# A hybrid decoder step on one core: the mixer's blocks in pairs, its small TensorE runs joined, the skip term on ScalarE

## The chip, the cores and the metric

One Trainium2 chip, one of its cores. The metric is device time in microseconds of one execution of the whole program, median over runs. TensorE multiplies matrices into PSUM, VectorE and ScalarE work on tiles in SBUF and PSUM, GpSimd (POOL) does small work and issues some DMAs, SyncE (SP) issues the rest.

## The reference

One layer of a decoder is applied to 256 prompt tokens and to 8 sample tokens (one new token each, with caches), with the same weights, all float32:

```
proj = rms_norm(x) @ w_in                  # q | k | v | z | x,B,C | dt, 6688 columns
attn = windowed GQA over 16 heads of 64, with q/k norm and per-head sinks
xbc  = silu(causal_dwconv(xbc, width 4))
y    = ssd_scan(xs, dt, a, B, C)           # two chunks of 128 tokens, 32 heads, state 128
y    = y + xs * d_skip                     # the skip term
y    = rms_norm(y * silu(z))
x    = x + concat(attn, y) @ w_out
x    = x + cross attention into 256 memory tokens
x    = x + conv FFN                        # 2048 -> 2 x 5632 -> 2048
```

Beside the two activations, the caches and states after the step are returned. For the sample tokens the scan is one step: y = C . (old state * decay) + ..., so each sample's old state (32 heads x 64 x 128) is multiplied by C and summed.

## The kernel before

Activations are kept transposed: 128 features on the partitions, 264 tokens (256 prompt, 8 sample) along the columns. Each large product is computed as three TensorE products of a high and a low part in the type fp32r (`mm3`, lines 104 to 106). Weights come in parts of 128 x 1024 on SP's queue; ScalarE writes the high part (line 89), VectorE the low part (line 90), four buffers each. `proj` accumulates two blocks of 128 output features at a time in two PSUM banks, both over the whole of a weight part before the next part, and then has each bank evacuated at high priority. There are three banks under the tag "mm", two under "t", one each under "s", "x" and "y".

The mixer is the stretch from the first input projection to the output projection. `in_pair` is called once per pair of 128-column blocks of w_in, 96 matmuls each, in the order k, v, q, B, C, x, z. Around these matmuls, the small work is issued:

- Scan decays (lines 477 to 506): cumulated log decays `la` come from a product with a triangle of ones, [128 tokens, 64]; a second pair of products, lines 481 and 482, computes the same transposed, 32 partitions wide, for a copy to DRAM (`dram_la`) that the scan later reads back broadcast.
- The sums of squares of q (lines 617 to 620): eight products, 32 outputs wide, go to four column groups of TensorE (`pq[32 * j:...]`).
- Attention of the first 128 queries (`attn_first`, four calls of two blocks each) and of the second 128 (`attn_prompt`, eight calls): logits, a softmax on VectorE and ScalarE, transposes, copy into `pt`, then value matmuls with 64 outputs (lines 602 and 564), copied to `attn`. Small fp32 products run as two passes each, so a call of four value matmuls shows 8 instructions.
- Sample attention (`attn_sample`): its small tiles `es_e` and `dgs` share the three buffers "h0" with the attention's probabilities and with the old states of `ssd_sample`.
- `conv_pair`: each evicted block goes into one of four single tiles `u` of a ring (`next_u`); the last 11 columns are copied to `cnew`, four taps are accumulated (line 748 on ScalarE, 750 on VectorE), then tanh.
- `ssd_prompt(g)`: for a group of 8 heads and each chunk: decays on ScalarE (814, 815), transposes of xs, value-like products (830, 64 outputs, 16 passes), the skip term and the sum on VectorE in four instructions (833), carry terms (838, 846).
- `ssd_sample(g)`: 8 loads of old states and 2 broadcasts on GpSimd's queue, 8 products (874) and 8 sums (875) on VectorE.
- `z_pair`: the gate, per block of 256 columns: tanh on ScalarE (905), two instructions on VectorE (906, 907), sum of squares, split into high and low part.

The order of work on every engine is made by a planner that simulates the engines and takes what is ready by priority, earlier in the program first. `issue_after(x)` holds the instructions of its block behind x on their engine. The engines then run their queues in order.

Of the kernel before, what the change touches and what calls it, by code (L numbers as in the profile page):

```python
# [7 lines left out]
F32 = mybir.dt.float32  # L8
F32R = mybir.dt.float32r
AF = mybir.ActivationFunctionType  # L10
ALU = mybir.AluOpType
# [5 lines left out]
TP, TS = 256, 8  # L17
T = TP + TS
# [30 lines left out]
def hybrid_decoder_step_kernel(ctx: ExitStack, tc: tile.TileContext, I, O):  # L49
    nc = tc.nc  # L50
# [10 lines left out]
    def psum(tag):  # L61
        return ps.tile([128, 512], F32, tag=tag, name=tag, bufs=banks[tag])
# [38 lines left out]
    marks = {}  # L101
# [166 lines left out]
    def pc(name, i=0, n=1):  # L268
        o = _PC[name][0]
        return par[:, o + i:o + i + n]  # L270
# [159 lines left out]
    p = psum("y")  # L430
# [49 lines left out]
    PE.matmul(p[:, 64:128], ones, dtan2, start=True, stop=True)  # L480
    for c in range(2):
        PE.matmul(p[0:32, 128 + c * 128:256 + c * 128], dtan[:, c, :], tri, start=True, stop=True)
    la = mp.tile([128, 64], F32, name="la")
# [9 lines left out]
    ring = []  # L493
    for i in range(4):
        u = mp.tile([128, 3 + T], F32, name=f"u{i}")
        P.memset(u[:, 0:3], 0.0)
        ring.append(u)
    ringn = [0]

    def next_u():  # L500
        ringn[0] += 1
        return ring[ringn[0] % 4]

    laT = next_u()[0:32, 3:259]
    V.tensor_copy(out=laT, in_=p[0:32, 128:384])
    nc.sync.dma_start(out=dram_la.rearrange("c h l -> h c l"), in_=laT.rearrange("p (c l) -> p c l", c=2))
    dsm = mp.tile([32, 2, 8], F32, name="dsm")
# [16 lines left out]

    def attn_prompt(j, rq, nrq, c):

# [29 lines left out]
        for h in range(2):  # L556
            for kb in range(nb):
                tr(p[:, (h * nb + kb) * 128:(h * nb + kb) * 128 + 128], e[:, h, kb * 128:kb * 128 + 128])
        pt = mp.tile([128, 4, 128], F32, tag="bc", name="pt", bufs=2)
        S.copy(out=pt[:, 0:2 * nb, :], in_=p[:, 0:2 * nk].rearrange("p (a q) -> p a q", q=128))  # L560
        o = psum("t")
        for h in range(2):
            for kb in range(nb):
                PE.matmul(o[64 * h:64 * h + 64, 0:128], vn[:, kb, pp, 64 * h:64 * h + 64], pt[:, h * nb + kb, :],
                          start=kb == 0, stop=kb == nb - 1)
        marks["attn"] = S.copy(out=attn[:, j, c * 128:c * 128 + 128], in_=o[:, 0:128])

    def attn_first(j):
# [28 lines left out]
        pt = mp.tile([128, 4, 128], F32, tag="bc", name="pt", bufs=2)  # L597
        S.copy(out=pt, in_=p.rearrange("p (a q) -> p a q", q=128))
        o = psum("t")
        for i in range(4):  # L600
            h = i % 2
            PE.matmul(o[64 * h:64 * h + 64, 128 * (i // 2):128 * (i // 2) + 128], vn[:, 0, pp, 64 * h:64 * h + 64], pt[:, i, :], start=True, stop=True)
        S.copy(out=attn[:, j:j + 2, 0:128], in_=o[:, 0:256].rearrange("p (i q) -> p i q", i=2))

# [12 lines left out]
    pq = psum("s")  # L617
    for d in range(2):
        for j in range(4):
            PE.matmul(pq[32 * j:32 * j + 32, 0:TP], nw[:, d, :], qsq[d][:, j, :TP], start=d == 0, stop=d == 1)  # L620
    cpc = mp.tile([128, 24, 8], F32, name="cpc")
# [28 lines left out]
    def second_chunk(pp):  # L650
# [6 lines left out]
        for h, (hs, ho) in enumerate(halves):  # L657
# [3 lines left out]
            V.tensor_tensor(out=qs[pp][ho, :, h, :], in0=x, in1=hi.bitcast(F32), op=ALU.subtract)  # L661

    for j in range(0, 8, 2):
        attn_first(j)
    for j in range(8):
        if j % 4 == 0:
            second_chunk(j // 4)
        d = 2 * (j // 4)
        attn_prompt(j, rqs[:, :, j % 4, d:d + 2], nrqs[:, :, j % 4, d:d + 2], 1)

    def attn_sample():
# [26 lines left out]
        S.activation(out=es, in_=sk, func=AF.Exp, bias=mx)  # L698
        e = mp.tile([128, 129], F32, tag="h0", name="es_e", bufs=3)
        S.activation(out=e, in_=p[:, 0:129], func=AF.Exp, bias=mx, accum_out=den)  # L700
# [5 lines left out]
        V.tensor_copy(out=zdiag(1)[:, :, :, 0:8], in_=p[:, 0:128].rearrange("p (j t c) -> p t j c", j=4, c=8))  # L706
        dg = mp.tile([128, 128], F32, tag="h0", name="dgs", bufs=3)
        V.tensor_scalar(out=dg, in0=ident, scalar1=e[:, 128:129], scalar2=None, op0=ALU.mult)
# [27 lines left out]

    def conv_blk(bi, pm):
        u = next_u()
        V.tensor_tensor(out=u[:, 3:], in0=pm, in1=r0, op=ALU.mult)
        return u  # L740

    def conv_side(b0, us, dst):
        c = mp.tile([128, 2, TP], F32, tag="c", name="c", bufs=2)
        for m, u in enumerate(us):
            bi = b0 + m
            V.tensor_copy(out=cnew[:, bi, :], in_=u[:, TP:])
# [18 lines left out]
    def conv_pair(b0, dst):  # L765
        us = []
        in_pair(lambda m, pm: us.append(conv_blk(b0 + m, pm)))
        conv_side(b0, us, dst)
# [28 lines left out]
    def ssd_prompt(g):  # L797
        hs = slice(8 * g, 8 * g + 8)
        hp = mp.tile([128, 512], F32, tag="hp", name="hp", bufs=1)
        for c in range(2):  # L800
# [31 lines left out]
            for i in range(4):  # L832
                V.scalar_tensor_tensor(out=x[:, i, :], in0=x[:, i, :], scalar=pc("d_skip", 4 * g + i), in1=y[:, i * 128:i * 128 + 128],
                                       op0=ALU.mult, op1=ALU.add)
            if c == 1:
# [54 lines left out]
    def z_pair(i):  # L890
        zs = []

        def ev(m, pm):
            z = next_u()[:, 3:]
            V.tensor_tensor(out=z, in0=pm, in1=r0, op=ALU.mult)
            V.tensor_copy(out=zsam[:, 2 * i + m, :], in_=z[:, TP:])
            zs.append(z[:, :TP])

        in_pair(ev)
        for m in range(2):  # L900
            k = 2 * i + m
            z = zs[m]
            y = xs[k // 4][:, k % 4, :TP]
            th = small.tile([128, T], F32, tag="raw", name="th")[:, :TP]
            S.activation(out=th, in_=z, func=AF.Tanh, scale=0.5)
            V.tensor_tensor(out=y, in0=z, in1=y, op=ALU.mult)
            V.scalar_tensor_tensor(out=y, in0=th, scalar=1.0, in1=y, op0=ALU.add, op1=ALU.mult)
            sumsq(accy[:, :TP], y, k == 0, TP, V)
            split(Y[k // 8][0][:, k % 8, :TP], Y[k // 8][1][:, k % 8, :TP], y, gssd[:, k:k + 1])
# [24 lines left out]

    conv_group(0)
    conv_group(1)
    ssd_prompt(0)
    conv_group(2)
    ssd_sample(0)
    ssd_prompt(1)  # L940
# [648 lines left out]
```

## Time and profile before

| | |
|---|---|
| median of 3 runs | 1386.8 us (1386.02 to 1387.09) |
| profiled execution | 1386.54 us, span 1384.3 us |
| TensorE busy | 1376.5 us, 99% of the span, 11415 matmuls |
| weight loads busy | 1348.3 us, 97% |
| VectorE busy | 1048.7 us, 76% |
| ScalarE busy | 766.1 us, 55% |
| GpSimd busy | 94.8 us, 7% |
| granted TensorE clock | full in all 40 slices |
| DMA | 298.31 MB, 215 GB/s in the mean |

Share is of the span. A fp32 product appears as two instructions per matmul; matmuls are pipelined, so an instruction's listed duration (some 0.28 us) is longer than the distance between two starts.

### The profile page before, as it was taken

To read this page: it belongs to the slowest core of one execution; us is meant where nothing else is said; L and a number is where in the kernel's file an instruction comes from. 1 tells how busy PE (TensorE), PEld (TensorE's weight loads), DVE (VectorE), ACT (ScalarE), POOL (GpSimd) and SP (SyncE) were. 2 spreads that over 40 slices of the span, in tenths; PEclk is the share of its full clock that TensorE was granted. 3 is DMA by queue.
4 is the path that set the end of the run, shared out by engine and by line. 5 is a ranking of instruction groups with operands and counts; after the bars stand their busy time and mean duration, and the time that the engine had idled before them with its cause. 6 is when DMAs were issued, how large, how long until landed. Compare 5 with 4: busy or idle time off the path is not lost.

```text
span 1384.3 us, 28768 instructions
## 1 busy us (share of the span) xinstructions
PE 1376.5 (99%) x11415; PEld 1348.3 (97%) x11415; DVE 1048.7 (76%) x1865; ACT 766.1 (55%) x1261; POOL 94.8 (7%) x286
## 2 busy tenths in 40 slices
PE   9999999999999999999999999999999999999999
PEld 8999999999999999889999999999999999999998
DVE  7979799999987774478777775777577757765655
ACT  7667755556545555476565544554455445543532
POOL 0000011111000000002010000000000000000000
PEclk9999999999999999999999999999999999999999
DMA  7954467777677566766576765676667656655664
GB/s 296 331 163 135 145 209 254 232 245 259 234 220 239 182 240 211 308 219 193 187 256 216 259 210 188 214 255 214 186 214 244 196 185 198 198 183 185 192 188 139
DMA packets 89477, 298.31 MB, mean 215 GB/s; under 512 B 12032, under 2 KB 17152, under 8 KB 88832
## 3 DMA queue, kind: packets, MB, share of 16 engines
q1 hardware_dynamic: 83840, 277.61, 60.6%
q0 software_dynamic: 5504, 18.88, 4.2%
q8 instruction: 89, 1.46, 0.4%
q14 instruction: 44, 0.36, 0.1%
HBM read 280.77 MB, written 16.23 MB: 215 GB/s over the span
## 4 chain that ended last, share of the span: by engine, by line
PE 97%; DMA 1%; DVE 1%; ACT 0%; issue 0%; SPq 0%; ACTq 0%
PE mm L105 21%; PE mm L104 20%; PE mm L106 20%; PE t L105 10%; PE t L106 9%; PE t L104 9%; PE t L245 1%; PE t L283 1%; PE y L830 1%; DMA wraw<-in_w_co_dram 1%; PE y L846 0%; DMA open<-in_open_dram 0%; PE x L283 0%; DVE wlo L90 0%; PE s L245 0%; PE mm L245 0%
## 5 line engine op out<-in xcount | busy, mean ns | idle before, releaser
L89 ACT CAST whi<-wraw 128x1024 fp32r<-128x1024 f32 x440 | 459.5, 1047 | 518.2 <-PE mm L105 278.3
L90 DVE TENSOR_TENSOR wlo<-wraw,whi 128x1024 fp32r<-128x1024 f32 x440 | 540.7, 1231 | 220.8 <-ACT whi L89 214.9
L105 PE MATMUL t<-x2l,whi 128*128 128x264 f32 x704 | 200.6, 285 | 0.0
L105 PE MATMUL mm<-x2l,whi 128*128 128x264 f32 x704 | 200.5, 285 | 0.0
L105 PE MATMUL mm<-hl,whi 128*128 128x264 f32 x704 | 199.6, 285 | 0.0
L106 PE MATMUL t<-x2h,wlo 128*128 128x264 f32 x704 | 199.1, 283 | 0.0
L106 PE MATMUL mm<-x2h,wlo 128*128 128x264 f32 x704 | 198.7, 283 | 0.0
L106 PE MATMUL mm<-hh,wlo 128*128 128x264 f32 x704 | 197.6, 282 | 0.0
L104 PE MATMUL mm<-x2h,whi 128*128 128x264 f32 x704 | 196.5, 279 | 0.4 <-DVE res L1285 0.4
L104 PE MATMUL t<-x2h,whi 128*128 128x264 f32 x704 | 196.4, 279 | 0.0
L104 PE MATMUL mm<-hh,whi 128*128 128x264 f32 x704 | 194.1, 280 | 0.0
L104 PE MATMUL mm<-xh,whi 128*128 128x264 f32 x576 | 163.8, 286 | 0.0
L105 PE MATMUL mm<-xl,whi 128*128 128x264 f32 x576 | 163.5, 285 | 0.0
L106 PE MATMUL mm<-xh,wlo 128*128 128x264 f32 x576 | 162.1, 286 | 0.0
L104 PEld LDWEIGHTS mm<-x2h,whi 128*128 128x128 f32 x704 | 132.3, 188 | 0.6 <-ACT whi L89 0.6
L104 PEld LDWEIGHTS t<-x2h,whi 128*128 128x128 f32 x704 | 132.3, 188 | 0.0
L106 PEld LDWEIGHTS t<-x2h,wlo 128*128 128x128 f32 x704 | 132.1, 188 | 0.0
L106 PEld LDWEIGHTS mm<-x2h,wlo 128*128 128x128 f32 x704 | 132.1, 188 | 0.0
L106 PEld LDWEIGHTS mm<-hh,wlo 128*128 128x128 f32 x704 | 131.9, 188 | 0.0
L105 PEld LDWEIGHTS mm<-hl,whi 128*128 128x128 f32 x704 | 131.7, 187 | 0.0
L105 PEld LDWEIGHTS mm<-x2l,whi 128*128 128x128 f32 x704 | 131.7, 187 | 0.0
L105 PEld LDWEIGHTS t<-x2l,whi 128*128 128x128 f32 x704 | 131.7, 187 | 0.0
(497 smaller groups left out, 2893.8 us busy)
## 6 DMA issues: line engine op xcount, KB each, us to landing
wraw<-in_w_up_dram SPq DMA_DIRECT2D x176, 512.0 KB, 4.4
wraw<-in_w_in_dram SPq DMA_DIRECT2D x96, 512.0 KB, 4.7
wraw<-in_w_dn_dram SPq DMA_DIRECT2D x88, 512.0 KB, 4.4
wraw<-in_w_out_dram SPq DMA_DIRECT2D x48, 512.0 KB, 4.3
h<-in_h_dram POOLq DMA_DIRECT2D x32, 256.0 KB, 4.6
hn<-in_h_dram SPq DMA_DIRECT2D x16, 512.0 KB, 4.8
out_state_s_dram<-hn POOLq DMA_DIRECT2D x16, 512.0 KB, 3.6
e<-dram_la SPq DMA_DIRECT2D x16, 256.0 KB, 4.8
```

Source lines behind the costliest of these rows:

```text
L89: S.copy(out=hi, in_=x)
L90: V.tensor_tensor(out=lo, in0=x, in1=hi.bitcast(F32), op=ALU.subtract)
L104: PE.matmul(out, wh, xh, start=start, stop=False)
L105: PE.matmul(out, wh, xl, start=False, stop=False)
L106: return PE.matmul(out, wl, xh, start=False, stop=stop)
L245: PE.matmul(first[c][:, :T], pre[k // 2][i][:, k % 2, c * 128:(c + 1) * 128], A[k // 8][x][:, k % 8, :], start=k + i + x == 0, stop=k == K ...
L283: return PE.transpose(out, in_, cst[0:k, C_ID:C_ID + k])
L830: PE.matmul(y[o:o + 64, (h // 2) * 128:(h // 2) * 128 + 128], xdt[:, h, :], es[h // 4][:, h % 4, :], start=True, stop=True)
```

## The change

- The two 32-wide products of line 482 go; `la` is transposed by TensorE instead ([128, 64] to [64, 128]) and that is copied to DRAM.
- The ring has two tiles of two blocks instead of four of one; evictions of a pair go into one tile. Copies to `cnew` and `zsam`, and the gate's tanh and VectorE instructions, handle both blocks at once. The gate's tanh tile has the tag "c" instead of "raw".
- The sums of squares of q are issued with the product that needs the last square first, the seven others behind it.
- `attn_first` and `attn_prompt` return `pt`; value matmuls of two calls are issued together, the one that needs the later `pt` first, the rest behind it, with one copy to `attn`. The `pt` of blocks 2, 3, 6 and 7 in the second half take the buffers "hp" and "cb" instead of "bc".
- The skip term: ScalarE scales xs by d_skip in place (four instructions), VectorE adds the PSUM bank in one.
- `es_e` and `dgs` become slices of a tile in the buffer "hp" instead of "h0".
- `ssd_sample(0)` comes right behind `conv_group(0)`, ahead of `conv_group(1)`; it stood behind `conv_group(2)`.

```diff
-    for c in range(2):
-        PE.matmul(p[0:32, 128 + c * 128:256 + c * 128], dtan[:, c, :], tri, start=True, stop=True)
...
-    for i in range(4):
-        u = mp.tile([128, 3 + T], F32, name=f"u{i}")
-        P.memset(u[:, 0:3], 0.0)
+    for i in range(2):
+        u = mp.tile([128, 2, 3 + T], F32, name=f"u{i}")
+        P.memset(u[:, :, 0:3], 0.0)
         ring.append(u)
...
-    laT = next_u()[0:32, 3:259]
-    V.tensor_copy(out=laT, in_=p[0:32, 128:384])
-    nc.sync.dma_start(out=dram_la.rearrange("c h l -> h c l"), in_=laT.rearrange("p (c l) -> p c l", c=2))
+    laT = next_u()[0:64, 0, 3:131]
+    p = psum("x")
+    tr(p[0:64, 0:128], la)
+    V.tensor_copy(out=laT, in_=p[0:64, 0:128])
+    nc.sync.dma_start(out=dram_la.rearrange("c h l -> (c h) l"), in_=laT)
...
+    def second_values(j, pts):
+        pp = j // 4
         o = psum("t")
...
+        def value(a, h, kb):
+            return PE.matmul(o[64 * h:64 * h + 64, 128 * a:128 * a + 128], vn[:, kb, pp, 64 * h:64 * h + 64], pts[a][:, 2 * h + kb, :],
+                             start=kb == 0, stop=kb == 1)
+
+        with tc.issue_after(value(1, 0, 0).ins):
+            for x in [(a, h, kb) for a in (1, 0) for h in range(2) for kb in range(2)][1:]:
+                value(*x)
+        marks["attn"] = S.copy(out=attn[:, j:j + 2, 128:TP], in_=o[:, 0:256].rearrange("p (i q) -> p i q", i=2))
...
+    def first_values(pp, pts):
...
+        with tc.issue_after(value(1, 0).ins):
+            for a, i in [(a, i) for a in (1, 0) for i in range(4)][1:]:
+                value(a, i)
+        S.copy(out=attn[:, 4 * pp:4 * pp + 4, 0:128], in_=o.rearrange("p (i q) -> p i q", i=4))
...
-    for d in range(2):
-        for j in range(4):
-            PE.matmul(pq[32 * j:32 * j + 32, 0:TP], nw[:, d, :], qsq[d][:, j, :TP], start=d == 0, stop=d == 1)
+
+    def q_sums(d, j):
+        return PE.matmul(pq[32 * j:32 * j + 32, 0:TP], nw[:, d, :], qsq[d][:, j, :TP], start=d == 1, stop=d == 0)
+
+    with tc.issue_after(q_sums(1, 3).ins):
+        for d in (1, 0):
+            for j in range(4):
+                if (d, j) != (1, 3):
+                    q_sums(d, j)
...
+    for pp in range(2):
+        first_values(pp, [attn_first(4 * pp + 2 * a) for a in range(2)])
     for j in range(0, 8, 2):
-        attn_first(j)
-    for j in range(8):
         if j % 4 == 0:
             second_chunk(j // 4)
         d = 2 * (j // 4)
-        attn_prompt(j, rqs[:, :, j % 4, d:d + 2], nrqs[:, :, j % 4, d:d + 2], 1)
+        second_values(j, [attn_prompt(x, rqs[:, :, x % 4, d:d + 2], nrqs[:, :, x % 4, d:d + 2], 1, tag)
+                          for x, tag in zip((j, j + 1), ("bc", "bc") if j % 4 == 0 else ("hp", "cb"))])
...
-                V.scalar_tensor_tensor(out=x[:, i, :], in0=x[:, i, :], scalar=pc("d_skip", 4 * g + i), in1=y[:, i * 128:i * 128 + 128],
-                                       op0=ALU.mult, op1=ALU.add)
+                S.activation(out=x[:, i, :], in_=x[:, i, :], func=AF.Copy, scale=pc("d_skip", 4 * g + i))
+            V.tensor_tensor(out=x, in0=x, in1=y.rearrange("p (i l) -> p i l", i=4), op=ALU.add)
...
+        zs = next_u()
+        in_pair(lambda m, pm: V.tensor_tensor(out=zs[:, m, 3:], in0=pm, in1=r0, op=ALU.mult))
+        V.tensor_copy(out=zsam[:, 2 * i:2 * i + 2, :], in_=zs[:, :, 3 + TP:])
+        z = zs[:, :, 3:3 + TP]
+        y2 = xs[i // 2][:, 2 * (i % 2):2 * (i % 2) + 2, :TP]
+        th = mp.tile([128, 2, TP], F32, tag="c", name="th", bufs=2)
+        S.activation(out=th, in_=z, func=AF.Tanh, scale=0.5)
+        V.tensor_tensor(out=y2, in0=z, in1=y2, op=ALU.mult)
+        V.scalar_tensor_tensor(out=y2, in0=th, scalar=1.0, in1=y2, op0=ALU.add, op1=ALU.mult)
...
     conv_group(0)
+    ssd_sample(0)
     conv_group(1)
     ssd_prompt(0)
     conv_group(2)
-    ssd_sample(0)
     ssd_prompt(1)
```

## Rows read from the trace of the kernel before

**Rows 1.** Stretches: us, then busy us (instructions) of PE, PEld, DVE, ACT, POOL; clock, DMA.

```profile
160.00:200.00 40.00, 40.00 (x383) 38.73 (x382) 31.46 (x76) 26.20 (x46) 4.47 (x8) 1.00 0.59 185
...
280.00:320.00 40.00, 40.00 (x337) 39.21 (x337) 40.00 (x85) 25.41 (x51) 6.86 (x7) 1.00 0.75 235
...
560.00:700.00 140.00, 137.10 (x1144) 130.91 (x1133) 102.82 (x177) 82.26 (x133) 12.92 (x33) 1.00 0.64 223
```

**Rows 2.** TensorE's waits: waited for, us in total, times, longest us; first of six.

```profile
PE x L206 <- DVE eps L279: 1.2, 1, 1.2
```

**Rows 3.** TensorE in order of time, a value run: start us, duration us, instruction, count.

```profile
107.49 0.28 PE L106 MATMUL mm<-xh,wlo 128*128 128x264 f32 x1
107.70 0.66 PE L602 MATMUL t<-pt,vn 128*64 128x128 f32 x8
...
108.52 0.28 PE L105 MATMUL mm<-xl,whi 128*128 128x264 f32 x1
```

**Rows 4.** TensorE in order of time, a run of 16 passes in the scan.

```profile
259.88 0.28 PE L105 MATMUL mm<-xl,whi 128*128 128x264 f32 x1
260.09 1.09 PE L830 MATMUL y<-e,xdt 128*64 128x128 f32 x16
...
261.34 0.28 PE L104 MATMUL mm<-xh,whi 128*128 128x264 f32 x1
```

**Rows 5.** TensorE in order of time, the sums of squares of q.

```profile
81.22 0.28 PE L106 MATMUL mm<-xh,wlo 128*128 128x264 f32 x1
81.43 1.06 PE L620 MATMUL s<-qsq,zz 128*32 128x256 f32 x12
...
82.64 0.29 PE L105 MATMUL mm<-xl,whi 128*128 128x264 f32 x1
...
83.37 0.28 PE L105 MATMUL mm<-xl,whi 128*128 128x264 f32 x1
...
84.35 0.29 PE L104 MATMUL mm<-xh,whi 128*128 128x264 f32 x1
```

**Rows 6.** TensorE in order of time, the log decays.

```profile
79.46 0.28 PE L104 MATMUL mm<-xh,whi 128*128 128x264 f32 x1
...
80.07 0.62 PE L482 MATMUL x<-cst,dtan 128*32 128x128 f32 x4
...
80.85 0.29 PE L106 MATMUL mm<-xh,wlo 128*128 128x264 f32 x1
```

**Rows 7.** TensorE in order of time, the transpose of a narrow tile.

```profile
155.09 0.28 PE L105 MATMUL mm<-xl,whi 128*128 128x264 f32 x1
155.21 0.27 PE L283 MATMUL x<-cst,bcs 128*32 128x128 f32 x1
...
155.44 0.28 PE L104 MATMUL mm<-xh,whi 128*128 128x264 f32 x1
```

**Rows 8.** VectorE from 70 to 420 us by line: busy us, mean ns, idle before.

```profile
L833 DVE SCALAR_TENSOR_TENSOR xs<-xs,par,y 128x128 f32<-128x128 f32 x32 | 9.1, 337 | 0.0
...
L907 DVE SCALAR_TENSOR_TENSOR xs<-th,xs 128x256 f32<-128x256 f32 x16 | 6.4, 410 | 0.0
...
L746 DVE COPY cnew<-u 128x11 f32<-128x11 f32 x24 | 3.9, 163 | 0.0
...
L843 DVE TENSOR_TENSOR ti<-y,ti 128x512 f32<-128x512 f32 x4 | 2.7, 677 | 0.0
```

**Rows 9.** ScalarE from 70 to 420 us by line, the scan's decays.

```profile
L814 ACT ACTIVATE e<-e,la 128x128 f32<-128x128 f32 x64 | 20.2, 391 | 17.0 <-DMA e<-dram_la 12.7 <-DVE xs L833 4.3
```

**Rows 10.** Old states of the samples, 160 to 260 us: waits ended by loads, landing times.

```profile
  DMA h<-in_h_dram: 0.9, 1
...
DMA to landing us min/median/max: 3.6/4.3/6.8
```

**Rows 11.** VectorE in order of time, the last gated sample rows.

```profile
412.61 0.35 DVE L97 TENSOR_TENSOR yl<-ysam,yh 128x64 fp32r<-128x64 f32 x2
```

**Rows 12.** TensorE in order of time, the second half of the output projection begins.

```profile
413.44 0.48 PE L104 MATMUL mm<-yh,whi 128*128 128x264 f32 x1
```

More of the change, by code (lines that the diff above doesn't have):

```diff
@@ L501, in next_u @@
         ringn[0] += 1
-        return ring[ringn[0] % 4]
-    laT = next_u()[0:32, 3:259]
-    V.tensor_copy(out=laT, in_=p[0:32, 128:384])
-    nc.sync.dma_start(out=dram_la.rearrange("c h l -> h c l"), in_=laT.rearrange("p (c l) -> p c l", c=2))
+        return ring[ringn[0] % 2]
+    laT = next_u()[0:64, 0, 3:131]
[3 more added lines that the diff above has]
+    nc.sync.dma_start(out=dram_la.rearrange("c h l -> (c h) l"), in_=laT)
     dsm = mp.tile([32, 2, 8], F32, name="dsm")
@@ L523, in hybrid_decoder_step_kernel, with attn_prompt @@
     V.tensor_scalar(out=nsink, in0=pc("sink_p", 0, 16), scalar1=-1.0, scalar2=None, op0=ALU.mult)
-    def attn_prompt(j, rq, nrq, c):
+    def attn_prompt(j, rq, nrq, c, tag):
         pp = j // 4
@@ L558, in attn_prompt @@
                 tr(p[:, (h * nb + kb) * 128:(h * nb + kb) * 128 + 128], e[:, h, kb * 128:kb * 128 + 128])
-        pt = mp.tile([128, 4, 128], F32, tag="bc", name="pt", bufs=2)
+        pt = mp.tile([128, 4, 128], F32, tag=tag, name="pt", bufs=2 if tag == "bc" else 1)
         S.copy(out=pt[:, 0:2 * nb, :], in_=p[:, 0:2 * nk].rearrange("p (a q) -> p a q", q=128))
+        return pt
+    def second_values(j, pts):
+        pp = j // 4
         o = psum("t")
[L562 to L566, printed above, removed]
+        def value(a, h, kb):
[5 more added lines that the diff above has]
+        marks["attn"] = S.copy(out=attn[:, j:j + 2, 128:TP], in_=o[:, 0:256].rearrange("p (i q) -> p i q", i=2))
     def attn_first(j):
@@ L598, in attn_first, with value @@
         S.copy(out=pt, in_=p.rearrange("p (a q) -> p a q", q=128))
+        return pt
+    def first_values(pp, pts):
         o = psum("t")
-        for i in range(4):
+        def value(a, i):
             h = i % 2
-            PE.matmul(o[64 * h:64 * h + 64, 128 * (i // 2):128 * (i // 2) + 128], vn[:, 0, pp, 64 * h:64 * h + 64], pt[:, i, :], start=True, stop=True)
-        S.copy(out=attn[:, j:j + 2, 0:128], in_=o[:, 0:256].rearrange("p (i q) -> p i q", i=2))
+            c = 256 * a + 128 * (i // 2)
+            return PE.matmul(o[64 * h:64 * h + 64, c:c + 128], vn[:, 0, pp, 64 * h:64 * h + 64], pts[a][:, i, :], start=True, stop=True)
+        with tc.issue_after(value(1, 0).ins):
+            for a, i in [(a, i) for a in (1, 0) for i in range(4)][1:]:
+                value(a, i)
+        S.copy(out=attn[:, 4 * pp:4 * pp + 4, 0:128], in_=o.rearrange("p (i q) -> p i q", i=4))
     qsq = [T3(apool, 4, tag="R", name=f"qsq{i}", bufs=4) for i in range(2)]
@@ L698, in attn_sample @@
         S.activation(out=es, in_=sk, func=AF.Exp, bias=mx)
-        e = mp.tile([128, 129], F32, tag="h0", name="es_e", bufs=3)
+        own = mp.tile([128, 512], F32, tag="hp", name="own", bufs=1)
+        e = own[:, 0:129]
         S.activation(out=e, in_=p[:, 0:129], func=AF.Exp, bias=mx, accum_out=den)
@@ L706, in attn_sample @@
         V.tensor_copy(out=zdiag(1)[:, :, :, 0:8], in_=p[:, 0:128].rearrange("p (j t c) -> p t j c", j=4, c=8))
-        dg = mp.tile([128, 128], F32, tag="h0", name="dgs", bufs=3)
+        dg = own[:, 256:384]
         V.tensor_scalar(out=dg, in0=ident, scalar1=e[:, 128:129], scalar2=None, op0=ALU.mult)
@@ L735, in hybrid_decoder_step_kernel @@
     cnew = mp.tile([128, 24, 11], F32, name="cnew")
[L737 to L740, printed above, removed]
     def conv_side(b0, us, dst):
         c = mp.tile([128, 2, TP], F32, tag="c", name="c", bufs=2)
-        for m, u in enumerate(us):
+        V.tensor_copy(out=cnew[:, b0:b0 + 2, :], in_=us[:, :, TP:])
+        for m in range(2):
+            u = us[:, m, :]
             bi = b0 + m
-            V.tensor_copy(out=cnew[:, bi, :], in_=u[:, TP:])
             w = [cwh[:, i * 24 + bi:i * 24 + bi + 1] for i in range(4)]
@@ L765, in conv_pair @@
     def conv_pair(b0, dst):
-        us = []
-        in_pair(lambda m, pm: us.append(conv_blk(b0 + m, pm)))
+        us = next_u()
+        in_pair(lambda m, pm: V.tensor_tensor(out=us[:, m, 3:], in0=pm, in1=r0, op=ALU.mult))
         conv_side(b0, us, dst)
@@ L890, in z_pair @@
     def z_pair(i):
[L891 to L899, printed above, removed]
+        zs = next_u()
[7 more added lines that the diff above has]
+        V.scalar_tensor_tensor(out=y2, in0=th, scalar=1.0, in1=y2, op0=ALU.add, op1=ALU.mult)
         for m in range(2):
             k = 2 * i + m
[L902 to L907, printed above, removed]
+            y = y2[:, m, :]
             sumsq(accy[:, :TP], y, k == 0, TP, V)
```

## The prediction

> **What bounds the kernel now.** I read the stretches first, then TensorE's waits, then the order of time around the places that the diff touches. In the stretches TensorE is busy for the whole 40.00 us of each of the 13 stretches from 40 to 560 us, of which two stand in [rows 1]; the mixer, which is all that the diff edits, lies inside. Busy alone proves little, since ends of matmuls are modelled. So I looked at the waits: the longest single wait of TensorE anywhere is 1.2 us, and none of its waits lies between 40 and 560 us [rows 2]. Then at starts in order of time: projection matmuls start 0.12 us apart there, and wherever the distance is larger, another TensorE instruction stands between. The mixer's length is therefore the sum of what TensorE issues. VectorE is second: 31.46 us busy of 40 in 160 to 200, but 40.00 in 280 to 320 [rows 1]. It is full there without delaying TensorE.
>
> What does cost TensorE something beside its columns is a change of shape. A run of value matmuls (output 64 partitions wide, 8 passes) begins 0.21 us after the last projection matmul instead of 0.12 [rows 3], and the first projection matmul behind it is stretched as well. So I price a run from the start of the last projection matmul ahead to the start of the second one behind, minus two steps of 0.12.
>
> **The change, part by part.**
>
> *Value runs.* One run of 8 passes: 108.52 - 107.49 - 0.24 = 0.79 us [rows 3]. A run of 16 passes of the same shape stands in the scan: 261.34 - 259.88 - 0.24 = 1.22 us [rows 4]. Two runs joined into one save 2 x 0.79 - 1.22 = 0.36. The first half of the queries has 4 runs and gets 2: 2 x 0.36 = 0.72 us. The second half has 8 and gets 4; nearly all of these 8 touch a run of transposes and share an end with it, which I put at 0.04 a run (no row prices it alone), so 4 x (2 x 0.75 - 1.22) = 1.1 us if the new ones stand alone and 4 x 0.36 = 1.4 if all do; I take 1.2. The run is ordered so that its first matmul needs the later of the two probability tiles; the rest is queued behind that one and cannot be split off.
>
> *Query sums.* Today these are three runs. The first (12 passes): 82.64 - 81.22 - 0.24 = 1.18. The second (2 passes): 84.35 - 83.37 - 0.24 = 0.74, and the third is its like at 85.9 us [rows 5]. Together 2.66. Eight products of 32 outputs go to four column groups, which work beside each other: the 12 passes are four rounds, the last two half full, and 16 passes fill the same four rounds. So I take 1.20 for the single run. Gain 1.46 us. The run now waits for the last square; what follows it (the norms of q) already waited for that.
>
> *Log-decay transposed.* The run at 79.46 us costs 80.85 - 79.46 - 0.24 = 1.15 us, of which the two 32-wide products hold everything from 80.07 on [rows 6]. Less the 0.09 that their own entry takes (0.21 - 0.12, as above), a projection matmul could start at 79.98 in their place and the next at 80.10: 80.10 - 79.46 - 0.24 = 0.40 us for what stays. The new transpose of `la` has its nearest row in that of `bcs`, 32 columns wide: 155.44 - 155.09 - 0.24 = 0.11 us, entered after 0.12 us like a projection matmul [rows 7]. I take that: gain 1.15 - 0.40 - 0.11 = 0.64. From the other side, if it changed shape as the value runs do, it costs 0.1 more on each side, gain 0.44. The Trainium skill says of this ("TensorEngine Tiling (Array Packing)", Key Properties) that changing the tiling mode drains the engine, which for an output of 64 partitions would be that 0.2; by it the sum below would be 3.8 instead of 4.0. The row disagrees for a transpose, the value runs agree. The transpose waits for VectorE's copy of `la` and takes its PSUM bank only when the three readers of the former tile are done; behind it waits only the DMA of `la` to DRAM, which is read for the decays of the scan, after attention.
>
> *Skip term, pairs, small copies: no TensorE time, priced as cover.* VectorE loses 32 instructions with 9.1 us and gets 8 additions of 512 columns at 0.68 (as the product from PSUM at line 843): -3.7 us. Copies into `cnew`: 24 become 12, -1.9; those into `zsam` 16 become 8 at the same rate, -1.1; the two gate instructions 16 become 8 each, 6.4 to about 5.4 for the second and a little less for the first, -1.6 [rows 8]. In all some 8 us less on VectorE. ScalarE gets 32 scalings of 128 columns; the decay rows are of that shape, 0.39 us each and 20.2 / 64 = 0.32 where they follow each other [rows 9], so 10 to 12.5 us. What hides this is the room on ScalarE, 25.41 us busy of 40 where VectorE is full [rows 1]. If the cover is gone, the price is a wait of the following VectorE addition behind ScalarE's queue; see the rivals.
>
> *Old states of group 0 ahead of the second convolution.* Same instructions, earlier: 8 products and 8 sums of about 0.68 us, 8 loads and 2 broadcasts on GpSimd's queue. The loads shared their buffers with the small tiles of the sample rows, and that wait goes. What is late next is the broadcast of C, whose one buffer now holds the probabilities of the seventh and eighth block. The earlier work falls into 160 to 200 us, where VectorE has 8.5 us free [rows 1]. Behind it in VectorE's order stand evictions and weight splits; behind it on GpSimd's queue, the first group's carry product and addition, needed only at the gate.
>
> *The ring of two double tiles* holds what four single ones held; the first half of a pair now also waits for readers of the other half, two pairs (2 x 96 x 0.12 = 23 us) earlier. Taken as nothing; bound: one eviction late by a VectorE instruction, 0.7 us, once.
>
> **Sum.** 0.72 + 1.2 + 1.46 + 0.64 = 4.0 us, against the profiled execution's own 1386.54 us (span 1384.3): 1382.5. The median of the runs is 0.26 above that execution, so 1382.8. The bounds above give 3.6 to 4.3. One split of the scan's 16-pass runs more or fewer (the last block has two runs of 8) moves it by 0.36 either way, and the 2.9 us that TensorE is idle in 560 to 700 us can move if the order on the engines comes out differently. The likeliest case's own range is thus 1381.0 to 1384.0.
>
> **Rivals.**
>
> *A: the gain comes back at the end of the mixer.* The second half of the output projection begins at 413.44 us [rows 12], and VectorE begins to deliver the last gated sample rows at 412.61 [rows 11]. If VectorE sets that moment, a TensorE that arrives 4.0 us sooner waits 4.0 - 0.8 = 3.2 us there, and the time is 1386.0. For: VectorE is full in 200 to 400. Against: its load falls by 8 us in that same stretch, and the runs that shrink lie before 170 us, where it has room.
>
> *B (slower): VectorE blocked on early states.* An in-order VectorE that waits for a state load holds up an eviction; two output banks follow each other, so an eviction may be 24 matmuls, 24 x 0.12 = 2.9 us, late before TensorE stops. The loads landed in 3.6 us at the least, 4.3 in the middle and 6.8 at worst [rows 10]. If all 8 moved products waited out the difference to the median, 8 x 2.5 = 20 us, less the 8.5 free, 11.5 us fall on TensorE; less 4.0: 1394.3. It decides from the point where a wait exceeds 2.9 us. Against: only one wait of 0.9 us for such a load stands in the stretch [rows 10]. The Trainium skill states a mechanism for late loads ("SBUF — State Buffer", the box on the "DVE blocks DMA" trap): descriptors of a DMA issued on GpSimd's queue are written by GpSimd, which is locked out while certain VectorE instructions run. The 6.8 in a stretch with VectorE full is in its favour, the median of 4.3 is not.
>
> *C (slower): VectorE's skip addition behind ScalarE.* ScalarE's queue holds weight conversions that wait for buffers. Were each of the 8 additions late enough to cost TensorE 1 us beyond those 2.9, the time is 1386.8 - 4.0 + 8 = 1390.8.
>
> *D: the edit does less than it says,* other TensorE work being set between the passes of a joined run, so that only sums and transpose gain: 2.1 us, 1384.7.
>
> **How the numbers follow.** Within 0.2% (2.8 us) nothing can be told from no change, so faster means below 1384.0, slower above 1389.6. Forecast 0.65; A 0.12 and D 0.09 fall inside 0.2%; B 0.06 and C 0.05 above; 0.03 for an order on the engines that changes stages the diff does not touch, either way. Faster 0.67, same 0.22, slower 0.11. The range reaches from 1380.8 over A and D to 1387.0 and leaves out B and C and the tails.
>
> **What would show it.** Right: value runs of 16 passes, 2 and 4 of them; one run of 16 for the query sums, near 1.2 us; no 32-wide product near 80 us; the first matmul of the up-projection and every later stage 4 us earlier, by the end of attention already; VectorE below 39 us in the 40 us stretches that were full. Wrong: a wait of TensorE between 40 and 560 us, above all on an eviction or on the last gated rows, or joined runs with projection matmuls between their passes.

## The result and the profile after

After: 1389.38 us median (12 runs, 1385.76 to 1392.04), before 1386.59 (12 runs, 1385.65 to 1387.12): ratio 1.0022, interval 1.0013 to 1.0030. The change made the kernel slower by 2.8 us where 4.0 less were forecast. The profiled execution of after, which the rows below describe, is the slowest of its runs: 1392.04 us, span 1389.8. The runs of after lie 6.3 us apart and those of before 1.5, so the waits below are those of one execution, 2.7 us above the median.

TensorE after, in order of time (start us, duration us, instruction, count): query sums with the transpose of `la`, then a joined value run, against [rows 3, 5 to 7].

```profile
83.78 0.28 PE L104 MATMUL mm<-xh,whi 128*128 128x264 f32 x1
83.91 0.27 PE L283 MATMUL x<-cst,la 128*64 128x128 f32 x1
83.93 0.37 PE L105 MATMUL mm<-xl,whi 128*128 128x264 f32 x1
84.23 1.07 PE L637 MATMUL s<-qsq,zz 128*32 128x256 f32 x16
85.23 0.39 PE L106 MATMUL mm<-xh,wlo 128*128 128x264 f32 x1
85.46 0.28 PE L104 MATMUL mm<-xh,whi 128*128 128x264 f32 x1
...
109.97 0.28 PE L104 MATMUL mm<-xh,whi 128*128 128x264 f32 x1
110.18 1.09 PE L615 MATMUL t<-pt,vn 128*64 128x128 f32 x16
...
111.43 0.28 PE L106 MATMUL mm<-xh,wlo 128*128 128x264 f32 x1
```

The first six rows hold three steps of 0.12 us: 85.46 - 83.78 - 0.36 = 1.32 us for the transpose and the sums (1.31 forecast). The value run costs 111.43 - 109.97 - 0.24 = 1.22, as forecast. At the last projection matmul ahead of the sample attention, TensorE is 4.76 us ahead of before (168.02 against 172.78; 0.44 of it from an earlier start). Compared at the same projection matmul, those that before issues at 170 to 175 us, after is 4.40 us ahead, 3.95 without its earlier start: the whole forecast gain. It is lost in the mixer. The stretches of after, columns as in [rows 1]:

```profile
160.00:200.00 40.00, 38.64 (x367) 37.02 (x366) 33.73 (x71) 25.63 (x45) 5.90 (x11) 1.00 0.63 209
200.00:240.00 40.00, 39.05 (x327) 37.12 (x327) 39.41 (x77) 21.99 (x43) 4.83 (x9) 1.00 0.72 242
240.00:280.00 40.00, 36.82 (x304) 35.34 (x302) 37.24 (x65) 23.30 (x44) 6.56 (x8) 0.98 0.72 221
280.00:320.00 40.00, 40.00 (x318) 38.33 (x319) 36.28 (x64) 24.40 (x46) 7.80 (x9) 0.93 0.62 202
```

TensorE is idle in three of them, and in 280 to 320 us it is busy with 318 matmuls instead of the 337 of [rows 1], at a granted clock of 0.93. Its waits between 150 and 420 us, where before has none [rows 2]:

```profile
PE mm L104 <- ACT whi L89: 3.2, 1, 3.2
PE mm L106 <- DVE wlo L90: 2.3, 3, 1.0
```

The three waits on the low part of a weight, at 185, 190 and 204 us, follow VectorE standing at the early state products. VectorE's stops of 160 to 260 us by what ended them, then VectorE in order of time:

```profile
DVE h L895 <- DMA cb<-dram_bc: 4.1, 2, 2.2
```

```profile
181.02 1.30 DVE L895 TENSOR_TENSOR h<-h,cb 128x512 f32<-128x512 f32 x2 [2.17 <-DMA cb<-dram_bc]
182.23 0.88 DVE L771 SCALAR_TENSOR_TENSOR c<-u,par,c 128x256 f32<-128x256 f32 x2
...
185.37 1.22 DVE L90 TENSOR_TENSOR wlo<-wraw,whi 128x1024 fp32r<-128x1024 f32 x1
...
197.51 1.29 DVE L895 TENSOR_TENSOR h<-h,cb 128x512 f32<-128x512 f32 x2 [1.88 <-DMA cb<-dram_bc]
```

TensorE meets that split (start us, duration us, instruction, and in brackets the idle time before it):

```profile
185.42 0.28 PE L105 MATMUL mm<-xl,whi 128*128 128x264 f32 x1
186.64 0.39 PE L106 MATMUL mm<-xh,wlo 128*128 128x264 f32 x1 [0.94 <-DVE wlo L90]
```

VectorE stands 2.17 us for the broadcast of C and then works off what is queued. The split begins at 185.37 and ends at 186.59, when TensorE has already stood for it 0.94 us. The longest wait comes through ScalarE, at the decays of the scan. ScalarE, then TensorE:

```profile
266.63 1.06 ACT L89 CAST whi<-wraw 128x1024 fp32r<-128x1024 f32 x1 [0.86 <-DMA wraw<-in_w_in_dram]
274.42 2.45 ACT L835 ACTIVATE e<-e,la 128x128 f32<-128x128 f32 x8 [6.73 <-DMA e<-dram_la]
276.77 1.03 ACT L89 CAST whi<-wraw 128x1024 fp32r<-128x1024 f32 x1
```

```profile
276.38 0.28 PE L105 MATMUL t<-xl,whi 128*128 128x264 f32 x1
279.84 0.59 PE L104 MATMUL mm<-xh,whi 128*128 128x264 f32 x1 [3.18 <-ACT whi L89]
280.23 0.42 PE L105 MATMUL mm<-xl,whi 128*128 128x264 f32 x1
280.45 0.42 PE L106 MATMUL t<-xh,wlo 128*128 128x264 f32 x1
```

ScalarE idles 6.73 us for a decay load; the eight decays run before the next weight conversion, which starts at 276.77, over 10 us after the one before. TensorE waits 3.2 us, and behind the wait its matmuls start 0.22 us apart instead of 0.12, at the lower level of its clock (1.2 of 2.4 GHz): the granted clock is 0.50 of full speed from 280 to 285 us, columns as in [rows 1].

```profile
280.00:285.00 5.00, 5.00 (x25) 4.76 (x27) 5.00 (x10) 3.44 (x8) 0.54 (x1) 0.50 0.38 120
```

It is full again from about 285.5 us on. Until then 19 projection matmuls and a run of 8 passes went at the lower level.

From 168.02 to the sum of squares that opens the second half of the output projection (419.02) after takes 251.0 us, before 240.4 (172.78 to 413.2). Of these 10.6 us the four waits are 6.1 (distances between starts, less 0.12), the matmuls at the low clock about 2.4, and the scan's value products in 12 runs against 9 about 1.1 (3 x 0.36); some 1 us is not traced to a row. The wait at 276 us with its low clock, 3.3 + 2.4 = 5.7 us, is the largest part; the three early waits are 2.8 us.

### The profile page after: what moved, and what is told of

It reads as the page before. It is cut to its first block, busy times and chain, and to the rows that moved or that the text cites. A ratio compares the mean times of both kernels' runs of the same rounds, so it can differ in the third digit from the quotient of the medians.

```text
span 1389.8 us, 28709 instructions
## 1 busy us (share of the span) xinstructions
PE 1377.1 (99%) x11412; PEld 1349.8 (97%) x11412; DVE 1043.6 (75%) x1805; ACT 773.5 (56%) x1279; POOL 92.3 (7%) x284
## 4 chain that ended last, share of the span: by engine, by line
PE 96%; DVE 1%; DMA 1%; ACT 1%; issue 1%; POOL 0%; DVEq 0%; ACTq 0%; POOLq 0%
PE mm L106 20%; PE mm L104 20%; PE mm L105 20%; PE t L106 10%; PE t L104 10%; PE t L105 9%; PE t L245 1%; DMA e<-dram_la 1%; PE y L851 1%; PE t L283 1%; PE y L867 0%; DMA cb<-dram_bc 0%; PE mm L245 0%; PE s L245 0%; PE x L283 0%
```

## The experiments

"Products" are the 32 multiplications of old states by C (line 874 before, 895 after), four groups of 8; their loads go through three buffers. Medians in us; each ratio is to before on the same chip. Several chips were used, and the median of before lay between 1386.1 and 1386.6 on them, so a difference of two runs from different chips is good to some 0.4 us. Parts of the change that a diff only names are those of the diff above.

**1. Single parts.**

*no_move*: only the place in the program undone.

```diff
-    ssd_sample(0)
     conv_group(1)
     ssd_prompt(0)
     conv_group(2)
+    ssd_sample(0)
```

> The changed kernel, but the old states of group 0 stand behind the third convolution again, as in the kernel before. Theory M (the moved old states: their broadcast of C has one buffer, lands late, and VectorE or ScalarE stand behind it): the waits of TensorE near 185, 190 and 204 us (3.0 us together) go, and if the late decay load at 276 us (3.3 us and the half clock behind it) came from the same crowding, that goes too; 1383 to 1384. Theory S (the skip term on ScalarE puts ScalarE's queue behind): nothing of the wait at 276 changes, 1386 to 1387. Theory R (the joined runs or the ring of pairs): 1389 as it is.

1389.47, ratio 1.0026 (1.0016 to 1.0035), the same as after: the planner takes what is ready, so the place in the program does nothing. The first product starts at 167 us either way, because the small tiles no longer hold its buffers.

*skip_dve*: the skip term back on VectorE.

```diff
-                S.activation(out=x[:, i, :], in_=x[:, i, :], func=AF.Copy, scale=pc("d_skip", 4 * g + i))
-            V.tensor_tensor(out=x, in0=x, in1=y.rearrange("p (i l) -> p i l", i=4), op=ALU.add)
+                V.scalar_tensor_tensor(out=x[:, i, :], in0=x[:, i, :], scalar=pc("d_skip", 4 * g + i), in1=y[:, i * 128:i * 128 + 128],
+                                       op0=ALU.mult, op1=ALU.add)
```

> The changed kernel, but the skip term is VectorE's again, in four instructions. Theory S: ScalarE reaches its decays and its weight conversions in time, the wait at 276 us goes, 1383 to 1385. Theory M: the waits on the broadcast of C stay, and VectorE has 3.7 us more to do in the full stretch, 1389 to 1391.

1387.3, 1.0009 (1.0 to 1.0018): 2.1 us of after come back, and the wait at 276 us is gone. Of the early waits the one at 185 us stays and is longer, 2.0 us idle instead of 0.94; those at 190 and 204 us are gone.

*runs_only*: before with the joined value runs, query sums and transposed `la`, nothing else.

> The kernel before with the TensorE runs alone changed: joined value runs, one run of query sums, la transposed. Theories M and S: no new wait of TensorE, so the gain of 4.0 us that the prediction summed comes out whole, 1382.6 (1382 to 1383.5). Theory R: the joined runs themselves make the engines late, 1386 or more.

1384.7, 0.9989 (0.9981 to 0.9998). Of some 4 us that TensorE issues less, 1.4 arrive; 1.7 us stand as two waits at 200 and 202 us, behind a 1.6 us stop of VectorE at a state load; some 0.9 us is not traced.

*move_only*: before with `ssd_sample(0)` ahead and `es_e`, `dgs` in "hp".

> The kernel before with the old states of group 0 ahead of the second convolution and the sample rows' small tiles in the buffer hp, nothing else. Theory M: waits of VectorE for the broadcast of C and waits of TensorE for weight parts between 180 and 290 us appear here too; 1389 to 1393. Theories S and R: 1386 to 1387, no wait of TensorE in that stretch.

1392.26, 1.0044 (1.0031 to 1.0056): the early states alone are the dearest single part, 6.1 us above before. Only 1.0 us of that are waits of TensorE at 185 to 209 us; its other waits, 3.0 us, lie between 177 and 394 us, 2.5 of them at 221 to 226. The scan's products come in one run more (0.36), and the rest is not traced.

*pairs_only*: before with ring, copies and gate in pairs.

> The kernel before with the blocks in pairs alone (ring of two double tiles, paired copies, paired gate). If fewer and larger instructions are only cover, as predicted: 1386 to 1387, no wait of TensorE. If the pair's one tile and the longer instructions hold up evictions or splits, as joined runs with pairs (1388.5) against joined runs alone (1384.7) suggest: 1388 to 1391.

1389.24, 1.0020 (1.0012 to 1.0029). This I had taken as nothing, with 8 us less on VectorE.

**2. Parts together.** *no_states* is after with the place and the small tiles undone; *runs_pairs* is that with the skip term on VectorE; *skip_runs* is runs_only with the skip term on ScalarE.

```diff
-        own = mp.tile([128, 512], F32, tag="hp", name="own", bufs=1)
-        e = own[:, 0:129]
+        e = mp.tile([128, 129], F32, tag="h0", name="es_e", bufs=3)
...
-        dg = own[:, 256:384]
+        dg = mp.tile([128, 128], F32, tag="h0", name="dgs", bufs=3)
```

> The changed kernel with both edits on the old states undone: group 0 behind the third convolution, and the sample rows' small tiles in the three buffers h0 again, so that the first state loads wait for them as before. Theory M2 (it is the freed buffers that let the states come 20 us earlier, and VectorE then stands at the broadcast of C): no wait of TensorE between 176 and 200 us, 2 to 3 us less than the changed kernel, 1386 to 1387.5; the decay wait near 276 us may stay. Theory S (the skip on ScalarE alone): as the changed kernel, 1389.

> The changed kernel with the old states as before and the skip term on VectorE: joined runs and blocks in pairs remain. If old states and skip are the two causes: 1383 to 1385, like the joined runs alone (1384.7) or a little less, since VectorE has some 4 us less to do. If the pairs (one ring tile for two blocks) cost something of their own: over 1386.

> The joined runs and the skip term on ScalarE, without pairs and with the old states as before. If the skip on ScalarE is relief for VectorE: 1383 to 1384.7. If ScalarE's queue then delays weight conversions (theory S): 1386 to 1388, with waits of TensorE for the high parts.

no_states 1386.5, 1.0001 (0.9992 to 1.0011): 2.9 us below after. That is what the pair of edits is worth on balance, and not the price of the early waits, for those are still there. The first product now starts at 179.2 us, VectorE stands 2.2 us at a state load ahead of 186.9, and TensorE waits 3.6 us between 190 and 206. What is gone is the wait at 276 us. TensorE's waits of no_states, 150 to 420 us:

```profile
PE mm L106 <- DVE wlo L90: 3.1, 3, 1.4
PE t L104 <- ACT whi L89: 0.6, 1, 0.6
```

runs_pairs 1388.47, 1.0013 (1.0005 to 1.0022). skip_runs 1384.58, 0.9987 (0.9978 to 0.9996). The skip term on ScalarE is thus worth nothing on runs_only, -2.0 us on runs_pairs and +2.1 beside the early states: single prices don't add.

**3. Which resource is late?** *resident* is after with C left out of the products: the broadcast is still loaded, but they take the tile `Bn`, already in SBUF, in its place. *decay_resident* is after with the 16 decay loads left out; ScalarE reads `Bn` in their place. *runs_free* and *runs_pool0* are runs_only with VectorE relieved.

```diff
 resident
-                V.tensor_tensor(out=h0, in0=h0, in1=cb, op=ALU.mult)
+                V.tensor_tensor(out=h0, in0=h0, in1=Bn[:, q, :, :], op=ALU.mult)
 decay_resident
-                nc.sync.dma_start(out=e, in_=dram_la[c, h0:h0 + 4, :].partition_broadcast(128))
...
-                        S.activation(out=e[:, j, :], in_=e[:, j, :], func=AF.Relu, scale=-1.0, bias=la[:, c * 32 + h0 + j:c * 32 + h0 + j + 1])
+                        S.activation(out=e[:, j, :], in_=Bn[:, c, j, :], func=AF.Relu, scale=-1.0, bias=la[:, c * 32 + h0 + j:c * 32 + h0 + j + 1])
 runs_free
+                if g == 0:
+                    V.tensor_tensor(out=ych[:, 4 * g + i, rows], in0=h0[:, :, 0], in1=cb[:, :, 0], op=ALU.mult)
+                    continue
 runs_pool0
-                V.tensor_tensor(out=h0, in0=h0, in1=cb, op=ALU.mult)
+                (P if g == 0 else V).tensor_tensor(out=h0, in0=h0, in1=cb, op=ALU.mult)
```

> The changed kernel, but the old states are multiplied with a tile that lies in SBUF (Bn) in place of the broadcast of C; the broadcast is still loaded, its result is left out of y. Theory M2: VectorE no longer waits for that load, the TensorE waits near 185, 190 and 204 us go, 1386 to 1387. If the state loads themselves are what is late, VectorE waits for those instead and nothing is gained: 1389.

1397.16, 1.0074 (1.0061 to 1.0087): not as expected. Freed of C, VectorE took the products sooner (the first at 155.1 us) and stood at the states themselves. The stop of 160 to 260 us, and TensorE's waits behind it:

```profile
DVE h L895 <- DMA h<-in_h_dram: 7.9, 5, 4.9
```

```profile
PE mm L106 <- DVE wlo L90: 6.3, 4, 4.8
```

> The changed kernel, but the decays are computed from a tile that lies in SBUF (Bn), and their 16 broadcast loads are left out. Theory D (ScalarE, in order, stands at a late decay load with weight conversions behind it): the wait of 3.3 us near 276 us and the half clock behind it, together some 6 us, go; 1383 to 1385. If the decays are not the cause: 1388 to 1389.

1386.12, 0.9996 (0.9988 to 1.0005): with the 16 decay loads gone, so are the wait at 276 us and 3.3 us of after; the early waits remain (1.9 us idle, against 2.3 in after).

> The joined runs alone, and in addition the 8 products and 8 sums of group 0's old states are left out on VectorE (a product of 8 columns stands for each, so that the loads and buffers stay). Theory V (TensorE, 4 us ahead by 170 us, overtakes VectorE's low-part splits, because VectorE is full from there on): with 9.7 us less on VectorE the two waits of TensorE at 200 and 202 us (1.7 us together) go and the summed gain comes out: 1382 to 1383. If TensorE's waits come from something else than VectorE's load: 1384.7 as the joined runs alone.

1387.93, 1.0011 (1.0002 to 1.002): with some 10 us of VectorE's work left out (8 products and 8 sums of 0.68, less what stays) it is slower than runs_only by 3 us. The theory that VectorE's load alone is the cause falls. Its one remaining instruction per state still stood at loads (5.6 us in three stops), now with an eviction behind it (a 1.9 us wait of TensorE at 189 us).

> The joined runs alone, with the 8 products of group 0's old states on GpSimd (some 2.3 us each there, as GpSimd's addition of the same size) and the sums still on VectorE. Theory V: VectorE has 4.8 us less in the tight stretch, 1382.5 to 1384. If GpSimd and VectorE hinder each other or VectorE's sums wait for the slower product: 1385 to 1387.

1393.45, 1.0048 (1.0035 to 1.006): not as expected; the sums on VectorE wait for GpSimd instead, and splits and an eviction behind them (four waits of TensorE of 0.9 to 2.8 us at 196 to 206, 6.8 together).

**4. Is it the edit, or the order?** Two edits of before that change no work: *null_bn* exchanges the transposes of B with the copies of the sample rows' B and C, *null_scan* writes the scan's transposes and VectorE products ahead of its decays.

> The kernel before with two independent blocks of the program exchanged: the transposes of B come behind the two small copies of the sample rows' B and C instead of ahead of them. Same instructions, same work; from 140 us on the planner orders the queues anew. The theory of late loads (an edit costs what a weight split or conversion waits behind a late load) has no price for it beyond 0.5 us: 1385.9 to 1386.9, unless a wait shows. The rival of the order (each new order of the full queues brings or removes waits of 1 to 3 us, whatever the edit is) expects over 1 us from before, up or down, with waits of TensorE between 180 and 420 us.

> The kernel before with the scan's transposes and value products on VectorE written ahead of its decays instead of behind them. Same instructions, same work, queues ordered anew from 200 us on. Theory of late loads: 1385.9 to 1386.9. Rival of the order: over 1 us from before in either direction.

null_scan 1386.54, 1.0003 (0.9994 to 1.0011). null_bn 1390.08, 1.0034 (1.0021 to 1.0047): as slow as the change itself, with no change of work. VectorE of null_bn, then TensorE's waits (150 to 420 us):

```profile
196.69 0.69 DVE L874 TENSOR_TENSOR h<-h,cb 128x512 f32<-128x512 f32 x1 [2.38 <-DMA h<-in_h_dram]
```

```profile
PE mm L106 <- DVE wlo L90: 2.1, 3, 1.2
PE t L104 <- ACT whi L89: 0.3, 1, 0.3
```

The three waits lie at 203.0, 205.4 and 207.3 us; those of pairs_only at 203.4, 205.4 and 207.3. In before the order happens to hide this spot: by the ends of the splits and the starts of the matmuls that use them, the closest split is ready 1.1 us ahead, in null_bn and in after 0.05. Before, then null_bn:

```profile
204.32 1.22 DVE L90 TENSOR_TENSOR wlo<-wraw,whi 128x1024 fp32r<-128x1024 f32 x1
206.59 0.28 PE L106 MATMUL mm<-xh,wlo 128*128 128x264 f32 x1
```

```profile
207.55 1.22 DVE L90 TENSOR_TENSOR wlo<-wraw,whi 128x1024 fp32r<-128x1024 f32 x1
208.83 0.39 PE L106 MATMUL mm<-xh,wlo 128*128 128x264 f32 x1 [1.22 <-DVE wlo L90]
```

**5. Holding the early products.** Group 0's 8 products are held on VectorE behind the last eviction of `conv_group(1)`; the call stands behind `conv_group(1)`.

```diff
-        in_pair(lambda m, pm: V.tensor_tensor(out=us[:, m, 3:], in0=pm, in1=r0, op=ALU.mult))
+        def ev(m, pm):
+            marks["ev"] = V.tensor_tensor(out=us[:, m, 3:], in0=pm, in1=r0, op=ALU.mult)
+        in_pair(ev)
...
-                V.tensor_tensor(out=h0, in0=h0, in1=cb, op=ALU.mult)
+                if g == 0:
+                    with tc.issue_after(marks["ev"].ins):
+                        V.tensor_tensor(out=h0, in0=h0, in1=cb, op=ALU.mult)
+                else:
+                    V.tensor_tensor(out=h0, in0=h0, in1=cb, op=ALU.mult)
```

> The kernel after, with the first group's 8 state products held on VectorE behind the last eviction of the second group's convolution (about 207 us) instead of starting at 167 us; loads as they come. Theory of late loads: the three waits of TensorE between 185 and 205 us (2.8 us) go, those at 276 us may stay: 1386.5 to 1387. Rival of the load (the same VectorE work falls where it is full, later): no better than after, 1389 or more, with waits between 210 and 260 us.

1382.33 (8 runs, 1381.9 to 1382.4), 0.9971 (0.9961 to 0.9982): 7.1 us under after, 3.9 under before, the fastest kernel here. The products start at 199.3 us (I had put that eviction at 207) and wait for no load. Its stretches, then the second half of the output projection:

```profile
160.00:200.00 40.00, 40.00 (x384) 38.88 (x383) 31.58 (x71) 26.70 (x46) 0.54 (x1) 1.00 0.54 172
...
240.00:280.00 40.00, 40.00 (x338) 38.42 (x337) 37.89 (x71) 25.31 (x50) 4.88 (x9) 1.00 0.76 239
280.00:320.00 40.00, 40.00 (x338) 38.42 (x337) 40.00 (x68) 25.20 (x49) 6.32 (x9) 1.00 0.77 247
```

```profile
409.43 0.61 PE L300 MATMUL y<-accy,cst 128*128 128x264 f32 x2
```

TensorE has no wait from 150 to 420 us, the clock is full, and the sum of squares starts at 409.4 against 413.2 before. Even the wait at 276 us is gone, more than I had expected.

The same hold on three others:

> The fastest so far (joined runs and the skip term on ScalarE), with the first group's 8 state products held behind the last eviction of the second group's convolution. Theory of late loads: its two waits at 200 and 202 us (1.7 us) go: 1382.9. Rival of the load: 11 us of VectorE work moved into its full stretch, waits after 210 us or at the last gated rows (413 us): 1385 to 1388.

> The kernel before with the blocks in pairs, which alone came to 1389.2 us, and the first group's 8 state products held behind the last eviction of the second group's convolution. If the price of the pairs is that of VectorE standing at the state loads near 200 us, the waits at 203 to 207 us (2.2 us) go and the time is that of before or a little less: 1385.5 to 1387. If the pairs have a price of their own (ring, double tiles): 1389.

> The exchange of two independent blocks, which alone came to 1390.1 us with no change of the work, with the same hold. If its price lies in the state loads near 200 us: the waits at 203 to 207 us (2.6 us) go, 1386 to 1388. If any new order of the queues brings waits of its own, others stand in their place after 210 us: 1388 to 1391.

skip_runs_held 1386.43, 1.0004 (0.9995 to 1.0013); pairs_held 1395.22, 1.0059 (1.0046 to 1.0072); null_bn_held 1396.63, 1.0073 (1.0059 to 1.0087). The early waits went in all three, and a late one came. TensorE's longest wait in null_bn_held, then that in pairs_held, which has a second one of 2.7 us behind ScalarE:

```profile
PE y L300 <- DVE accy L927: 8.2, 1, 8.2
```

```profile
PE y L300 <- DVE accy L922: 3.2, 1, 3.2
```

The 32 products are one long chain through three buffers, and its last sum is needed by the gate of the sample rows, whose squares open the second half of the output projection. From the starts in order of time (us; waits are distances between starts, less 0.12):

| kernel | first product | last sum | TensorE's waits, 185 to 209 | wait for the squares | median |
|---|---|---|---|---|---|
| before | 186.3 | 389.4 | 0 | 0 | 1386.6 |
| after | 167.2 | 352.1 | 2.8 | 0 | 1389.4 |
| after_held | 199.3 | 386.2 | 0 | 0 | 1382.3 |
| runs_only | 180.0 | 383.2 | 1.7 | 0 | 1384.7 |
| move_only | 167.3 | 341.9 | 1.0 | 0 | 1392.3 |
| no_states | 179.2 | 371.8 | 3.6 | 0 | 1386.5 |
| runs_pairs | 178.9 | 375.7 | 2.1 | 0 | 1388.5 |
| skip_runs | 180.1 | 368.0 | 1.8 | 0 | 1384.6 |
| skip_runs_held | 199.1 | 395.1 | 0 | 0.8 | 1386.4 |
| pairs_only | 184.7 | 381.8 | 2.2 | 0 | 1389.2 |
| pairs_held | 203.6 | 404.8 | 0 | 3.2 | 1395.2 |
| null_bn | 184.3 | 388.0 | 2.6 | 0 | 1390.1 |
| null_scan | 186.3 | 386.4 | 0.2 | 0 | 1386.5 |
| null_bn_held | 203.2 | 409.5 | 0 | 8.2 | 1396.6 |

Every chain in the table that starts before 186 us comes with early waits, and every one that ends after 390 delays the squares. The changed kernel had 37 us in hand at its end (352.1 against 389.4) and paid for them at its start. Holding pays where the chain behind is short: from first product to last sum 187 us in after_held, but 201 in pairs_held and 206 in null_bn_held.

The hold moves two things together, VectorE's stops at the loads and its own work on the products and sums. runs_free has the stops without most of the work and still loses. In runs_pairs VectorE stands only 1.1 us at loads in the stretch in which TensorE waits 2.1, so the stops alone hardly explain it. No run here separates the two.

## Why the prediction was wrong

- *TensorE's sum* (4.0 us) was right, term by term, and after_held shows it whole: 3.9 us against before on the same chip, 1382.33 beside 1382.8 forecast. For the transpose the row of the narrow one held; the drain of the Trainium skill ("TensorEngine Tiling (Array Packing)", Key Properties) does not appear at this output of 64 partitions.
- *"The earlier work falls into 160 to 200 us, where VectorE has 8.5 us free"*, costed at nothing: this step failed. Room in a stretch is no cover when the work must wait for a load inside an in-order queue. VectorE's idle time was there (33.73 busy of 40), but in front of the product, with the splits behind it. VectorE stood 4.1 us at two products, the low parts behind them came late, and TensorE waited 2.8 us at 185 to 205 us. With the products held these waits are gone in all four kernels that had them, and after_held is 7.1 us under after. I listed what stood behind the products, evictions and weight splits, and priced only evictions, with their 2.9 us of slack; the splits had as little as 1.1.
- *What is late next is the broadcast of C*: named rightly, not priced. It is the load in both stops, 2.17 and 1.88 us.
- *The wait at 276 us* is the largest single loss in the profile of after, 5.7 us with its low clock, and the sum had no term for it: a decay load ahead of a weight conversion on ScalarE's queue. It is absent when the early states are undone (no_states), when they are held (after_held), with the skip term back on VectorE (skip_dve), and without the decay loads (decay_resident). Of the kernels run here only after and no_move (2.1 us) show it, and both have the early states and the skip term on ScalarE together; resident has both too and does not show it. Why those loads were late is open.
- *Skip term, priced as cover*: no cost by itself; with the early states it cost 2.1 us (skip_dve), and the wait at 276 us came with it. VectorE's total fell by 5.1 us (1048.7 to 1043.6; 8 forecast), and that helped nothing there. It may be what let after_held end its chain in time; no run separates that.
- *Ring "taken as nothing"*: pairs_only cost 2.8. The spot is that of null_bn, so the price need not be the ring's; pairs_held traded it for another wait, so whether the pairs have a price of their own stays open.
- *Joined runs* were right in size, but with TensorE 4 us earlier every deadline on weights moves up by as much; runs_only lost 1.7 of it at once.
- *Rivals.* B had mechanism and place, with the wrong thing behind the product (splits, not evictions) and four times the size. A, dismissed by VectorE's load, is what three of the four held kernels met. C did not occur: the skip addition held nobody. D did not occur: all six value runs have their 16 passes.
- *Chance 0.03 for another order on the engines*: far too small. null_bn moved the time by 3.9 us with no work changed. How much of every single price above is that order stays open, since only null edits and one spot were measured.

## What to carry to other kernels

Before pricing an edit of a queue as covered, list for the engine that feeds the critical one how far ahead its deliveries are at the closest (here the weight splits, 1.1 us), and which loads its in-order queue may stand at just ahead of them. A long chain of loads and small products has a window: start it late enough that no load is awaited, early enough that its end is not. When a planner orders full queues, run one or two edits that change no work first: what they move is the unit for reading single edits.

## What the runs showed of the hardware

Loads of the same size took up to twice as long to land in one order of the queues as in another. DMA issues of 255 to 280 us, before and then after (KB each, median us to landing):

```profile
e<-dram_la SPq DMA_DIRECT2D x4, 256.0 KB, 5.2
cb<-dram_bc POOLq DMA_DIRECT2D x1, 256.0 KB, 5.0
out_conv_new_dram<-cnew SPq DMA_DIRECT2D x1, 132.0 KB, 4.5
```

```profile
e<-dram_la SPq DMA_DIRECT2D x2, 256.0 KB, 9.1
cb<-dram_bc POOLq DMA_DIRECT2D x1, 256.0 KB, 8.6
out_conv_new_dram<-cnew SPq DMA_DIRECT2D x1, 132.0 KB, 9.2
```

The two decay loads and the broadcast of C of after were issued within 0.44 us of each other, from 265.27 us on. More traffic is not what the rows show: in 255 to 280 us after moved 6.12 MB at 245 GB/s, before 6.65 MB at 266. At 267 to 269 us, with all of these loads under way, the DMA engines were 36% busy; in before, behind decay loads, 95%. The stretch of after, columns as in [rows 1] (before's is 262 to 264 us):

```profile
267.00:269.00 2.00, 2.00 (x19) 2.00 (x18) 2.00 (x5) 0.69 (x1) 0.00 (x0) 1.00 0.36 91
```

In after_held decay loads issued at 267 us took 7.1 to 7.5 us and TensorE waited for nothing. The mechanism that rival B takes from the Trainium skill ("SBUF — State Buffer", the box on the "DVE blocks DMA" trap) is about DMAs issued on GpSimd's queue; loads issued on SP's queue were as late here, so it cannot by itself account for them. Whether it delayed the broadcast of C, no run separates.

Behind TensorE's wait of 3.2 us in after, matmuls ran at the lower level of the clock until about 285.5 us, so that wait cost about 5.7 us in all: 3.3, and the 2.4 that the slower matmuls took longer.
